# HGRN scores in bursts of two levels, with decayed keys and queries alternating between two pairs of tiles

## The chip, the cores and the metric

The kernel runs on one core of a Trainium2 chip. The metric is the device time of one execution in microseconds. Engines are called as the profile calls them: PE (TensorE, with PEld for its weight loads), DVE (VectorE), ACT (ScalarE), POOL (GpSimd), SP (SyncE, which issues the DMAs).

## The reference

One decoder layer is computed for a prompt of 1024 new tokens and for 8 sequences that decode one token each. RMSNorm, one input projection, then two mixers side by side: HGRN2 (8 heads, key and value width 128) and Mamba-2; an output projection with residual; RMSNorm and a gated MLP; a final RMSNorm. The part that the change touches is one HGRN head over the prompt. With forget gates f, keys k = 1 - f, queries q and values v:

```python
b = jnp.cumsum(g, axis=2)                                  # g = log f
o = jnp.einsum('bhtk,bhkv->bhtv', q * jnp.exp(b), S)
diff = b[:, :, :, None, :] - b[:, :, None, :, :]
decay = jnp.exp(jnp.where(causal, diff, -jnp.inf))
A = jnp.einsum('bhtsk,bhsk->bhts', decay * q[:, :, :, None, :], k)
o = o + jnp.einsum('bhts,bhsv->bhtv', A, v)
S_new = jnp.exp(b_last[:, :, 0])[..., None] * S + jnp.einsum('bhsk,bhsv->bhkv', k * jnp.exp(b_last - b), v)
```

The decay between two positions differs in each of the 128 key channels, so the scores A are no plain product of q and k. All data is float32.

## The kernel before, in words

The layer runs in one program. PE executes in the order in which the program is written; the order of DVE, ACT, POOL and of the DMA queues is made by a planner at build time, which follows data dependencies and takes earlier-written work first. On each engine the instructions then run in that order.

**Two interleaved streams.** Projections are jobs in a list (`in_job`, `out_job`). A job of a head is one of its four inputs f, q, v and sg (the output gate): 3 chunks of 344 columns times 24 matmuls, 72 steps of one matmul, each step a `yield`. A head's recurrence (`head`, L810) is a generator too; it yields weights. `drive` walks through the head's generator and for a weight w runs w x left / 32 steps of the projection jobs, where left is 4 jobs x 72 = 288. While head h is worked on, the four projections of head h+1 run in between; for the last head the output jobs o8.0 to o12.2 run instead, with residual tiles transposed in between. What the generator leaves of the four jobs runs behind its last piece. The weights thus set how many projection matmuls stand between two pieces of a head, and PE keeps that order.

**The scores of one head.** T = 1024 positions lie along the free axis of q, k and f (128 channels on the partitions); they are cut into 8 chunks of 128. Pairs of positions at distance zero, then within blocks of 2, 4, 8, ... are scored level by level. `near` (L851) issues the scores of a level as 32 small matmuls, 32 columns of k by 32 of q, each into a 32-partition strip of a PSUM bank; on PE each is two instructions. `scale(lv)` (L840) then multiplies the first half of every block of 2 x 2^lv keys by the second half's decay, and the second half of the queries by the first half's decay, in place, and forms the decays of the doubled blocks (tiles `tt`). The order written is: a yield of 2 (head 0: 5), the transposes of v (`vtp`, L872), level "a0" with undecayed q; q = q*f on DVE (L876) and the diagonal into `amc` (L877); then for lv = 0 to 3 a score burst `a1`, `scale(lv)` (L845, L846, L848), and a predicated copy of that level's scores into `amc` (L887); inside lv = 3, after two more units, a burst 16 columns wide and `scale(4)`. Then four ACT copies of `amc` into the block matrix `am` (L890), burst `a5` (16 matmuls), `scale(5)` and ACT copies (L896), burst `a6` (8 matmuls of 64 x 64), `scale(6)` and a copy (L902). A level's matmuls read k and q, the next `scale` writes them in place, so each level waits for the one before on PE and on DVE in turn.

**What follows in a head.** `od` is the readout of the eight decode states (its decode states `Sh` are prepared on DVE L828 and POOL L827 and L829, its queries `qb` L819), copied to `odr` (L911). `ktp` transposes the decayed keys (L917), `kv` forms chunk states that DVE accumulates (L929, L931), `o` forms the outputs, `hms` and `dms` their norms. Before all of it stands `vd` (L815), the transpose of v's 8 decode columns, which DVE copies (L817) and SP stores and reloads.

**Buffers.** f, k, q, v and sg are tiles of the ring "big" (10; head 0's f is in "e", 2). Half tiles (`vt`, `kt`, `tt`, `SS`, `sq`, `amc`) come from the ring "s" (11). Score banks come from a ring of four PSUM banks "mx"; `vd`, `od`, `odp`, `dms` and the norm sums `ms` of the Mamba stage share one bank "nx".

**What lies beside it.** Weight tiles are split into a high and a low part on ACT (`wh`, L183) and DVE (`wl`, L184) at each job's start. Projection results leave PSUM through ACT (L799), f further through L792 and k through DVE L793. In head 0 the Mamba gate's norm is still finished on DVE (L638 to L640, L683). In head 7 the mixer outputs are split for the output jobs (L984 on ACT, L985 on DVE) and residuals are added (L769).

Of the kernel before, what the change touches and what calls it, by code (L numbers as in the profile page):

```python
# [12 lines left out]
ALU = mybir.AluOpType  # L13
# [3 lines left out]
P = 128  # L17
# [33 lines left out]
def hybrid_layer(  # L51
# [19 lines left out]
    def nm(s):  # L71
        cnt[0] += 1
        return f"{s}_{cnt[0]}"
# [12 lines left out]
    def half(name):  # L86
        return tl("s", name)[:, :512]
# [722 lines left out]
    def head(h, t):  # L810
        f, k, q, v, sg = (t[n] for n in ("f", "k", "q", "v", "sg"))


        dps = bank("vd", "nx")
        PE.transpose(dps[:ND, :P], v[:, T:NT], ident)  # L815
        vd = small.tile([ND, P], F32, tag="vd", name=nm("vd"))
        V.tensor_copy(vd, dps[:ND, :P])  # L817
        SP.dma_start(vd_d[h], vd)
        V.tensor_tensor(qb[:, :, 0:ND], eye8, q[:, T:NT].unsqueeze(2).to_broadcast([P, ND, ND]), op=ALU.mult)  # L819
        Sds = []  # L820
        for b0 in (0, 4):
            bs = slice(b0, b0 + 4)
            ds = slice(T + b0, T + b0 + 4)
            Sd, vb = tl("ld", "Sh"), tl("d", "vb")[:, :512]
            fetch(d4(Sd), state_hgrn[0, bs, h].rearrange("b k v -> k b v"))
            fetch(vb, vd_d[h, bs].rearrange("b n -> (b n)").unsqueeze(0).to_broadcast([P, 512]))
            G.tensor_tensor(d4(vb), d4(vb), cb(k[:, ds]), op=ALU.mult)  # L827
            V.tensor_tensor(d4(Sd), d4(Sd), cb(f[:, ds]), op=ALU.mult)  # L828
            G.tensor_tensor(Sd, Sd, vb, op=ALU.add)  # L829
            SP.dma_start(hgrn_sample[0, bs, h].rearrange("b k v -> k b v"), d4(Sd))  # L830
            Sds.append(d4(Sd))


        hb = [slice(0, 512), slice(512, T)]
        qa, ka, fa = q[:, :T], k[:, :T], f[:, :T]
        vt, kt, SS, sq = ([None, None] for _ in range(4))
        tts = [half("tt"), half("tt")]
        Tc = fa

        def scale(lv):  # L840
            nonlocal Tc
            hh, nb = 1 << lv, 512 >> lv
            q4, k4 = (t.rearrange("p (n two h) -> p n two h", two=2, h=hh) for t in (qa, ka))
            T3 = Tc.rearrange("p (n two) -> p n two", two=2)
            V.tensor_tensor(k4[:, :, 0, :], k4[:, :, 0, :], T3[:, :, 1:2].to_broadcast([P, nb, hh]), op=ALU.mult)  # L845
            V.tensor_tensor(q4[:, :, 1, :], q4[:, :, 1, :], T3[:, :, 0:1].to_broadcast([P, nb, hh]), op=ALU.mult)  # L846
            Tn = tts[0] if lv == 0 else tts[1][:, 512 - (1024 >> lv):512 - (512 >> lv)]
            V.tensor_tensor(Tn, T3[:, :, 0], T3[:, :, 1], op=ALU.mult)  # L848
            Tc = Tn

        def near(ps, s0, t0, n, step):  # L851

            for c in range(NC):
                for b in range(0, P, step):
                    c0 = c * P + b
                    mm(ps[b + s0:b + s0 + n, c * 32 + t0:c * 32 + t0 + n], k[:, c0 + s0:c0 + s0 + n],
                       q[:, c0 + step - n:c0 + step])

        def c32(t):
            return t.rearrange("p (c t) -> p c t", t=32)  # L860

        def m32(m):
            return m.unsqueeze(1).to_broadcast([P, NC, 32])


        amc = half("amc")[:, :256]
        yield 2.0 if h else 5.0
        for hf in range(2):
            vt[hf] = half("vt")
            ps = bank("vtp")  # L870
            for i in range(4):
                PE.transpose(ps[:, blk[i]], v[:, hf * 512 + i * P:hf * 512 + (i + 1) * P], ident)  # L872
            A.copy(vt[hf], ps)
        ps = bank("a0")
        near(ps, 0, 0, 32, 32)
        V.tensor_tensor(qa, qa, fa, op=ALU.mult)  # L876
        V.tensor_tensor(c32(amc), c32(ps[:, :256]), m32(eyec), op=ALU.mult)  # L877
        yield 2.5
        for lv in range(4):
            ps = bank("a1")  # L880
            near(ps, 0, 0, 32, 32)
            scale(lv)
            if lv == 3:
                yield 2.0
                near(ps, 0, 16, 16, 32)
                scale(4)
            V.copy_predicated(c32(amc), m32(mlow[:, lv, :]), c32(ps[:, :256]))  # L887
            yield 2.2 if lv else 2.6
        for g in range(4):
            A.copy(am[32 * g:32 * g + 32, :, 32 * g:32 * g + 32], c32(amc)[32 * g:32 * g + 32])  # L890

        ps = bank("a5")
        near(ps, 0, 0, 32, 64)
        scale(5)
        for b in (0, 64):
            A.copy(am[b:b + 32, :, b + 32:b + 64], c32(ps[:, :256])[b:b + 32])  # L896
        yield 2.0
        ps = bank("a6")
        for c in range(NC):
            mm(ps[0:64, c * 64:(c + 1) * 64], k[:, c * P:c * P + 64], q[:, c * P + 64:(c + 1) * P])  # L900
        scale(6)
        A.copy(am[0:64, :, 64:P], ps[0:64, :].rearrange("p (c t) -> p c t", t=64))  # L902
        yield 1.8


        ops = bank("od", "nx")
        for b in range(ND):
            g = b % 4
            mm(ops[32 * g:32 * g + 32, :P], qb[:, b, :], Sds[b // 4][:, b % 4, :], start=(b < 4), stop=(b >= 4))
        odr = small.tile([P, P], F32, tag="odr", bufs=1, name=nm("odr"))  # L910
        V.tensor_copy(odr, ops[:, :P])  # L911

        for hf in range(2):
            kt[hf] = half("kt")
            ps = bank("ktp")
            for i in range(4):
                PE.transpose(ps[:, blk[i]], k[:, hf * 512 + i * P:hf * 512 + (i + 1) * P], ident)  # L917
# [525 lines left out]
```

## Time and profile before

| | |
|---|---|
| median of 3 runs | 1794.77 us (1794.24 to 1795.13) |
| the profiled execution | 1793.98 us, span 1791.7 us |
| busy share of the span | PE 97%, PEld 94%, DVE 63%, ACT 44%, POOL 23% |
| the eight heads | about 384 to 900 us of the span |
| one steady head | 62.0 us |

Times in a trace count from the start of the span. A row of the timeline has start, time, engine, line, operation, output tile and input tiles, shapes and count, and in brackets the idle time before it and what ended it. A row of the chain of waits has start, time and what the chain ran through, with a count of instructions. A row of the waits names who waited for whom, the microseconds in total, the times and the longest. A row of the stretches gives busy microseconds of each engine with instruction counts, the granted PE clock and the DMA share. Matmuls are pipelined, so their durations overlap; the distance from start to start is what one costs PE.

### The profile page before, as it was taken

To read this page: it belongs to the slowest core of one execution; us is meant where nothing else is said; L and a number is where in the kernel's file an instruction comes from. 1 tells how busy PE (TensorE), PEld (TensorE's weight loads), DVE (VectorE), ACT (ScalarE), POOL (GpSimd) and SP (SyncE) were. 2 spreads that over 40 slices of the span, in tenths; PEclk is the share of its full clock that TensorE was granted. 3 is DMA by queue.
4 is the path that set the end of the run, shared out by engine and by line. 5 is a ranking of instruction groups with operands and counts; after the bars stand their busy time and mean duration, and the time that the engine had idled before them with its cause. 6 is when DMAs were issued, how large, how long until landed. Compare 5 with 4: busy or idle time off the path is not lost.

```text
span 1791.7 us, 38454 instructions
## 1 busy us (share of the span) xinstructions
PE 1735.9 (97%) x16143; PEld 1678.5 (94%) x16143; DVE 1124.0 (63%) x2011; ACT 793.1 (44%) x1416; POOL 406.7 (23%) x415
## 2 busy tenths in 40 slices
PE   7999999999999999999999988999999999999998
PEld 6998899998999999999899978999999999999997
DVE  6667966565554555557746769666666667555545
ACT  7577688453444344345323344333433334111114
POOL 2113322120110110111100364455444542000001
PEclk9999999999999999999999998999999999999999
DMA  4144734642221222234333431222222225422212
GB/s 154 39 126 125 192 106 126 183 136 97 72 79 50 84 74 70 66 96 149 93 118 121 140 108 48 95 72 72 79 84 87 72 72 198 151 90 96 96 60 95
DMA packets 218019, 182.34 MB, mean 102 GB/s; under 512 B 13388, under 2 KB 195158, under 8 KB 217830
## 3 DMA queue, kind: packets, MB, share of 16 engines
q1 hardware_dynamic: 217558, 179.80, 32.6%
q8 instruction: 126, 2.06, 0.5%
q14 instruction: 47, 0.39, 0.1%
q0 software_dynamic: 288, 0.10, 0.0%
HBM read 141.53 MB, written 38.52 MB: 100 GB/s over the span
## 4 chain that ended last, share of the span: by engine, by line
PE 81%; DVE 7%; ACT 4%; DMA 3%; issue 2%; POOL 1%; SPq 0%; DVEq 0%; POOLq 0%; ACTq 0%
PE mm L93 34%; PE ub L93 14%; PE dn L93 14%; PE ua L93 10%; PE a L93 2%; PE o L93 1%; DMA csb<-cs_d 1%; ACT csb L530 1%; PE kv L93 1%; DVE ml L985 1%; DMA ml<-mix_d 1%; DVE wl L184 1%; DVE xbc L334 1%; DMA ws<-in_w_in_dram 1%; ACT L531 1%
## 5 line engine op out<-in xcount | busy, mean ns | idle before, releaser
L93 PE MATMUL mm<-hh,wh 128*128 128x344 f32 x1248 | 407.6, 327 | 0.0
L93 PE MATMUL mm<-hl,wh 128*128 128x344 f32 x1248 | 405.9, 326 | 0.0
L93 PE MATMUL mm<-hh,wl 128*128 128x344 f32 x1248 | 404.3, 324 | 0.0
L93 PEld LDWEIGHTS mm<-hh,wh 128*128 128x128 f32 x1248 | 236.2, 190 | 3.5 <-issue 0.9
L93 PEld LDWEIGHTS mm<-hl,wh 128*128 128x128 f32 x1248 | 236.2, 189 | 2.6 <-issue 0.9
L93 PEld LDWEIGHTS mm<-hh,wl 128*128 128x128 f32 x1248 | 236.2, 189 | 2.3 <-issue 1.0
L183 ACT CAST wh<-ws 128x1024 fp32r<-128x1024 f32 x96 | 100.5, 1047 | 259.8 <-PE dn L93 130.9
L93 PE MATMUL ub<-ul,wh 128*128 128x258 f32 x704 | 200.1, 284 | 4.3 <-DVE ul L1130 4.3
L93 PE MATMUL ub<-uh,wh 128*128 128x258 f32 x704 | 200.4, 285 | 2.0 <-ACT uh L1129 2.0
L93 PE MATMUL ub<-uh,wl 128*128 128x258 f32 x704 | 200.6, 285 | 0.0
L93 PE MATMUL dn<-ah,wh 128*128 128x256 f32 (+1 forms) x640 | 181.2, 283 | 0.9 <-DVE x L1373 0.9
L93 PE MATMUL dn<-al,wh 128*128 128x256 f32 (+1 forms) x640 | 180.5, 282 | 0.0
L93 PE MATMUL dn<-ah,wl 128*128 128x256 f32 (+1 forms) x640 | 180.1, 281 | 0.0
L184 DVE TENSOR_TENSOR wl<-ws,wh 128x1024 fp32r<-128x1024 f32 x96 | 125.7, 1310 | 49.6 <-ACT wh L183 47.4
L93 PE MATMUL mm<-mh,wh 128*128 128x258 f32 x512 | 148.0, 289 | 9.0 <-DVE x L1026 8.9
L93 PE MATMUL ua<-ul,wh 128*128 128x258 f32 x528 | 149.2, 282 | 0.9 <-DVE ul L1130 0.9
L93 PE MATMUL ua<-uh,wh 128*128 128x258 f32 x528 | 148.8, 282 | 0.0
L93 PE MATMUL ua<-uh,wl 128*128 128x258 f32 x528 | 148.4, 281 | 0.0
L93 PE MATMUL mm<-ml,wh 128*128 128x258 f32 x512 | 146.3, 286 | 0.3 <-DVE ml L985 0.3
L93 PE MATMUL mm<-mh,wl 128*128 128x258 f32 x512 | 146.1, 285 | 0.0
L93 PEld LDWEIGHTS ub<-ul,wh 128*128 128x128 f32 x704 | 134.5, 191 | 5.0 <-DVE ul L1130 5.0
L93 PEld LDWEIGHTS ub<-uh,wh 128*128 128x128 f32 x704 | 134.2, 191 | 2.5 <-ACT uh L1129 2.5
(333 smaller groups left out, 3914.5 us busy)
## 6 DMA issues: line engine op xcount, KB each, us to landing
ws<-in_w_in_dram SPq DMA_DIRECT2D x52, 512.0 KB
ws<-in_w_up_dram SPq DMA_DIRECT2D x44, 512.0 KB
ws<-in_w_out_dram SPq DMA_DIRECT2D x24, 512.0 KB
act_d<-val SPq DMA_DIRECT2D x22, 516.0 KB
al<-act_d SPq DMA_DIRECT2D x22, 516.0 KB
ws<-in_w_down_dram SPq DMA_DIRECT2D x22, 512.0 KB
ml<-mix_d SPq DMA_DIRECT2D x48, 172.0 KB
csb<-cs_d SPq DMA_DIRECT2D x32, 256.0 KB
```

The costliest lines, as they stand in the source:

```text
L93: PE.matmul(out, lhsT, rhs, start=start, stop=stop)
L183: A.copy(wh[:, :n], ws[:, :n])
L184: V.tensor_tensor(wl[:, :n], ws[:, :n], wh[:, :n].bitcast(F32), op=ALU.subtract)
L334: V.scalar_tensor_tensor(acc[:, :n], ext[:, q:q + n], col(wname, q * ntile + j), acc[:, :n], op0=ALU.mult, op1=ALU.add)
L530: A.activation(csb3[:, h, :], csb3[:, h, :], AF.Relu, scale=-1.0, bias=cst[:, h0 + h:h0 + h + 1])
L531: A.activation(csb, csb, AF.Exp, scale=-1.0)
L985: V.tensor_tensor(lo[:, cols], x_, hi[:, cols].bitcast(F32), op=ALU.subtract)
```

## The change

Decayed keys and queries have two pairs of tiles, (k, v) and (f, q). The transposes of v move to the head's start, right behind `vd`, so that v is free; q*f is written to v ahead of the first yield. `scale(lv, x_, y_)` reads pair x_ and writes pair y_; where they differ, ACT copies the halves that are not multiplied. A group of the score stage is now two levels: a0 with level 0, level 1 with level 2, level 3 with its 16-wide part, level 5 with level 6; `od` follows level 6 in the same group. Levels 1, 3 and 5 write to the other pair. `ktp` reads f, which holds the final keys, and stands behind a yield of its own. Six copies of 128 x 512 per head are new on ACT; the numbers of matmuls, of DVE products and of DMAs do not change. The weights of a head sum to 28.2 before and after (head 0: 31.2 and 30.7).

```diff
         PE.transpose(dps[:ND, :P], v[:, T:NT], ident)
+        vt = [half("vt"), half("vt")]
+        for hf in range(2):
+            ps = bank("vtp")
+            for i in range(4):
+                PE.transpose(ps[:, blk[i]], v[:, hf * 512 + i * P:hf * 512 + (i + 1) * P], ident)
+            A.copy(vt[hf], ps)
...
-        Tc = fa
-        def scale(lv):
+        Tc = f[:, :T]
+        pair = [(k[:, :T], v[:, :T]), (f[:, :T], q[:, :T])]
+        def scale(lv, x_, y_):
...
+            V.tensor_tensor(ky[:, :, 0, :], kx[:, :, 0, :], T3[:, :, 1:2].to_broadcast([P, nb, hh]), op=ALU.mult)
+            V.tensor_tensor(qy[:, :, 1, :], qx[:, :, 1, :], T3[:, :, 0:1].to_broadcast([P, nb, hh]), op=ALU.mult)
+            if x_ is not y_:
+                A.copy(ky[:, :, 1, :], kx[:, :, 1, :])
+                A.copy(qy[:, :, 0, :], qx[:, :, 0, :])
...
+        def level(lv, ps):
+            V.copy_predicated(c32(amc), m32(mlow[:, lv, :]), c32(ps[:, :256]))
...
-        yield 2.0 if h else 5.0
+        V.tensor_tensor(pair[0][1], q[:, :T], f[:, :T], op=ALU.mult)
+        yield 2.5 if h else 5.0
+        p0, p1 = bank("a0"), bank("a1")
+        near(p0, (k, q), 0, 0, 32, 32)
+        near(p1, pair[0], 0, 0, 32, 32)
+        scale(0, pair[0], pair[0])
+        scale(1, pair[0], pair[1])
+        V.tensor_tensor(c32(amc), c32(p0[:, :256]), m32(eyec), op=ALU.mult)
+        level(0, p1)
+        yield 4.5
+        p0, p1 = bank("a1"), bank("a2")
+        near(p0, pair[0], 0, 0, 32, 32)
+        near(p1, pair[1], 0, 0, 32, 32)
+        scale(2, pair[1], pair[1])
+        scale(3, pair[1], pair[0])
+        level(1, p0)
+        level(2, p1)
+        yield 4.5
+        ps = bank("a3")
+        near(ps, pair[1], 0, 0, 32, 32)
+        near(ps, pair[0], 0, 16, 16, 32)
+        scale(4, pair[0], pair[0])
+        scale(5, pair[0], pair[1])
+        level(3, ps)
         for g in range(4):
             A.copy(am[32 * g:32 * g + 32, :, 32 * g:32 * g + 32], c32(amc)[32 * g:32 * g + 32])
+        yield 4.5
+        ps, p6 = bank("a5"), bank("a6")
+        near(ps, pair[0], 0, 0, 32, 64)
+        for c in range(NC):
+            mm(p6[0:64, c * 64:(c + 1) * 64], f[:, c * P:c * P + 64], q[:, c * P + 64:(c + 1) * P])
+        scale(6, pair[1], pair[1])
         for b in (0, 64):
             A.copy(am[b:b + 32, :, b + 32:b + 64], c32(ps[:, :256])[b:b + 32])
+        A.copy(am[0:64, :, 64:P], p6[0:64, :].rearrange("p (c t) -> p c t", t=64))
         ops = bank("od", "nx")
...
         V.tensor_copy(odr, ops[:, :P])
+        yield 3.5
...
-                PE.transpose(ps[:, blk[i]], k[:, hf * 512 + i * P:hf * 512 + (i + 1) * P], ident)
+                PE.transpose(ps[:, blk[i]], f[:, hf * 512 + i * P:hf * 512 + (i + 1) * P], ident)
```

More of the change, by code (lines that the diff above doesn't have):

```diff
@@ L834, in head @@
         hb = [slice(0, 512), slice(512, T)]
-        qa, ka, fa = q[:, :T], k[:, :T], f[:, :T]
-        vt, kt, SS, sq = ([None, None] for _ in range(4))
+        kt, SS, sq = ([None, None] for _ in range(3))
         tts = [half("tt"), half("tt")]
-        Tc = fa
-        def scale(lv):
+        Tc = f[:, :T]
+        pair = [(k[:, :T], v[:, :T]), (f[:, :T], q[:, :T])]
+        def scale(lv, x_, y_):
             nonlocal Tc
             hh, nb = 1 << lv, 512 >> lv
-            q4, k4 = (t.rearrange("p (n two h) -> p n two h", two=2, h=hh) for t in (qa, ka))
+            (kx, qx), (ky, qy) = ([t.rearrange("p (n two h) -> p n two h", two=2, h=hh) for t in z] for z in (x_, y_))
             T3 = Tc.rearrange("p (n two) -> p n two", two=2)
-            V.tensor_tensor(k4[:, :, 0, :], k4[:, :, 0, :], T3[:, :, 1:2].to_broadcast([P, nb, hh]), op=ALU.mult)
-            V.tensor_tensor(q4[:, :, 1, :], q4[:, :, 1, :], T3[:, :, 0:1].to_broadcast([P, nb, hh]), op=ALU.mult)
+            V.tensor_tensor(ky[:, :, 0, :], kx[:, :, 0, :], T3[:, :, 1:2].to_broadcast([P, nb, hh]), op=ALU.mult)
[3 more added lines that the diff above has]
+                A.copy(qy[:, :, 0, :], qx[:, :, 0, :])
             Tn = tts[0] if lv == 0 else tts[1][:, 512 - (1024 >> lv):512 - (512 >> lv)]
@@ L849, in scale, with near @@
             Tc = Tn
-        def near(ps, s0, t0, n, step):
+        def near(ps, kq, s0, t0, n, step):
+            kk, qq = kq
             for c in range(NC):
@@ L855, in near @@
                     c0 = c * P + b
-                    mm(ps[b + s0:b + s0 + n, c * 32 + t0:c * 32 + t0 + n], k[:, c0 + s0:c0 + s0 + n],
-                       q[:, c0 + step - n:c0 + step])
+                    mm(ps[b + s0:b + s0 + n, c * 32 + t0:c * 32 + t0 + n], kk[:, c0 + s0:c0 + s0 + n],
+                       qq[:, c0 + step - n:c0 + step])
         def c32(t):
@@ L863, in m32 @@
             return m.unsqueeze(1).to_broadcast([P, NC, 32])
+        def level(lv, ps):
+            V.copy_predicated(c32(amc), m32(mlow[:, lv, :]), c32(ps[:, :256]))
         amc = half("amc")[:, :256]
-        yield 2.0 if h else 5.0
[L868 to L888, printed above, removed]
+        V.tensor_tensor(pair[0][1], q[:, :T], f[:, :T], op=ALU.mult)
@@ L889, in head @@
+        scale(3, pair[1], pair[0])
[8 more added lines that the diff above has]
+        level(3, ps)
         for g in range(4):
             A.copy(am[32 * g:32 * g + 32, :, 32 * g:32 * g + 32], c32(amc)[32 * g:32 * g + 32])
-        ps = bank("a5")
-        near(ps, 0, 0, 32, 64)
-        scale(5)
+        yield 4.5
@@ L895, in head @@
+        ps, p6 = bank("a5"), bank("a6")
[3 more added lines that the diff above has]
+        scale(6, pair[1], pair[1])
         for b in (0, 64):
             A.copy(am[b:b + 32, :, b + 32:b + 64], c32(ps[:, :256])[b:b + 32])
[L897 to L900, printed above, removed]
@@ L901, in head @@
-        scale(6)
-        A.copy(am[0:64, :, 64:P], ps[0:64, :].rearrange("p (c t) -> p c t", t=64))
-        yield 1.8
+        A.copy(am[0:64, :, 64:P], p6[0:64, :].rearrange("p (c t) -> p c t", t=64))
         ops = bank("od", "nx")
```

## The prediction

> **What bounds the kernel now.** I read the page's busy shares first, then the waits of PE, then the chain of waits through one HGRN head, then the timeline of PE at one score burst.
>
> ```profile
> PE 1735.9 (97%) x16143; PEld 1678.5 (94%) x16143; DVE 1124.0 (63%) x2011; ACT 793.1 (44%) x1416; POOL 406.7 (23%) x415
> 646.00:708.00 62.00, 62.00 (x810) 59.30 (x809) 34.63 (x63) 27.30 (x42) 8.27 (x6) 1.00 0.24 71
> PE a L93 <- DVE q L846: 8.2, 4, 4.2
> PE ms L93 <- DVE vd L817: 1.8, 1, 1.8
> ```
>
> The second row is one period of a steady head (columns: PE, PEld, DVE, ACT, POOL busy, granted clock, DMA share): PE is never idle in its 62 us, at full clock, while DVE works 34.6 and ACT 27.3. So in heads 1 to 6 only PE's own time counts. All waits of PE in the eight heads that matter are the last two rows: four for decayed queries (one of 4.2 us in head 0, the others, 4.0 together, in head 7) and one at head 0's start. The chain through this period shows what PE's time is made of:
>
> ```profile
> 641.37 5.52 PE mm L93 x35
> 646.88 0.11 PE vd L815
> ...
> 649.83 0.87 PE vtp L872 x8
> 650.70 0.69 PE a L93 x50
> 651.39 3.66 PE mm L93 x22
> ...
> 682.82 0.57 PE od L93 x16
> 683.39 1.02 PE ktp L917 x8
> ```
>
> An undisturbed projection matmul costs 5.52/35 = 0.158 us. Between them stand ten groups on narrow columns of the array: vd, eight score bursts (a0, shown right behind vtp, and levels 0 to 3, each of 64 instructions; then the 16-wide half, level 5, level 6) and od. What one costs shows in the timeline of PE (start, time, instruction):
>
> ```profile
> 654.57 0.32 PE L93 MATMUL mm<-hh,wl 128*128 128x344 f32 x1
> 654.73 0.32 PE L93 MATMUL mm<-hh,wh 128*128 128x344 f32 x1
> 654.99 0.76 PE L93 MATMUL a<-q,k 128*32 128x32 f32 x64
> 655.68 0.43 PE L93 MATMUL mm<-hl,wh 128*128 128x344 f32 x1
> 655.94 0.32 PE L93 MATMUL mm<-hh,wl 128*128 128x344 f32 x1
> L93 PE MATMUL a<-q,k x3456: 176/196/270, 395.3 to 869.7; 128*32 128x32 f32 x160, 128*16 128x16 f32 x32
> ```
>
> The burst starts 0.26 us after the last projection instead of 0.158 (0.10 lost). Its 64 instructions span 0.76 and each lasts 0.196 (last row, median), so the last starts 0.56 after the first: 0.009 apiece. The next projection starts at 0.69, 0.13 after that, and its successor 0.26 later, 0.10 over the pitch. **The edges of a burst cost 0.10 + 0.13 + 0.10 = 0.33 us, its matmuls 0.56.** A level that joins another's burst saves 0.33.
>
> **The change, part by part.** The matmuls are the same in number and shape. A unit of a yield is 288/32 = 9 projection steps, 1.42 us, and the yields of a head sum to 28.2 units before and after (head 0: 31.2 and 30.7), so only the grouping changes. (2.5 units are 22 steps, as in the row of 22 projections behind a0.)
>
> *Score groups.* Joined are a0 with level 0, level 1 with 2, level 3 with the 16-wide half: 3 x 0.33 = 0.99 us per head. Level 5, level 6 and od also run together, but with the array's columns going 32, 64, 32 inside. The trace has no such direct turn; the nearest are the full group's turns to and from narrow columns:
>
> ```profile
> 649.66 1.04 PE L872 MATMUL vtp<-ident,v 128*128 128x128 f32 x8
> 650.63 0.36 PE L93 MATMUL a<-q,k 128*32 128x32 f32 x20
> ...
> 682.75 0.65 PE L93 MATMUL od<-Sh,qb 128*32 128x128 f32 x16
> 683.32 1.09 PE L917 MATMUL ktp<-ident,k 128*128 128x128 f32 x8
> ```
>
> From 649.66, eight transposes at 0.87/8 = 0.109 would have ended at 650.53; the burst starts at 650.63, so a turn costs 0.10 there. Each of the two joints then saves between 0 (the turn costs a whole edge) and 0.33; I take 0.15, nearer to the 0.10 row with something for the tail: 0.30 per head. Against it, od no longer turns straight into ktp but back to a projection, at 0.13 + 0.10; the present turn takes some 0.2 of the 0.57 between their starts, so I put a loss of 0.06 (0 to 0.33). The vtp transposes move from a0 to vd: both cost 0.87 either way. Sum: 0.99 + 0.30 - 0.06 = **1.23 us per head** (0.7 to 1.6).
>
> The Trainium skill, TensorEngine Tiling, Key Properties, says that changing the tiling mode drains TensorE. The 0.33 agrees with a drain at each change; by that rule the two inner joints change the mode too and save nothing, and the sum would be 2 us smaller over the heads.
>
> *Waits between bursts.* Before, each level waited for PE, then had about 3.4 us. Now two levels have 4.5 units, 6.4 us, and their second half may come 0.26 + 0.56 later: 7.2 us from the end of a burst for two k and two q products, two merges and whatever else DVE does. The rows of the present period, first the stretch that becomes window one (DVE shares it with POOL's decode products), then what falls in window two:
>
> ```profile
> 655.79 1.10 DVE L845 TENSOR_TENSOR k<-k,f 128x512 f32<-128x512 f32 x1 [0.52 <-PE a L93]
> 656.81 1.78 DVE L846 TENSOR_TENSOR q<-q,f 128x512 f32<-128x512 f32 x1
> 660.29 1.11 DVE L845 TENSOR_TENSOR k<-k,tt 128x512 f32<-128x512 f32 x1 [1.34 <-PE a L93]
> 661.33 0.68 DVE L846 TENSOR_TENSOR q<-q,tt 128x512 f32<-128x512 f32 x1
> 661.93 0.44 DVE L887 COPY_PREDICATED amc<-mlow,a 128x256 f32<-128x256 uint8 x1
> 662.83 1.23 DVE L184 TENSOR_TENSOR wl<-ws,wh 128x1024 fp32r<-128x1024 f32 x1 [0.46 <-ACT wh L183]
> 664.47 0.70 DVE L793 TENSOR_SCALAR k<-f 128x1032 f32<-128x1032 f32 x1 [0.41 <-ACT f L792]
> 656.42 1.62 POOL L829 TENSOR_TENSOR Sh<-Sh,vb 128x512 f32<-128x512 f32 x1
> L873 ACT COPY vt<-vtp x16: 586/589/595, 395.0 to 836.8; 128x512 f32<-128x512 f32 x16
> ```
>
> Window one: 1.10 + 1.78 + 1.11 + 0.68 for the products, 2 x 0.44 for the two merges, 0.7 for one product of decays (128x512 too): 6.2 us. Window two: 4 x 0.69, 0.88, 1.23, 0.70: 5.6. Both are under 7.2.
>
> New on ACT are two copies of 128x512 for each of three levels, the halves that the level does not scale. No row has such a strided copy from one buffer to another; the nearest is the 0.59 of vt, so 6 x 0.59 = 3.5 us per head on an engine with 35 us to spare. If one must wait for the DVE product beside it, it ends 0.6 after DVE: 6.8 of 7.2 in window one. That is thin, and I charge 0.3 us per head for it in heads 1 to 6 (0 to 1.2). The product q*f now goes to v, after the transposes of v: emitted 2.5 units (3.5 us) ahead of the burst that reads it; its 1.2 to 1.4 us (twice a 128x512 product) are hidden by those projections, and uncovered would cost as much a head.
>
> Buffers: v and f are held to level 5 and to ktp, k is freed sooner; the ring of ten holds two heads of five tiles, and the next writer comes a head later, so nothing. Decode outputs: od's inputs come from POOL's L829, at work at 656 (the row above), and od moves only from 682.8 to near 676; its earlier copy to odr and selod matmul stay behind kv. No DMA is added, and vd's store and SP's queue keep their place; the vt copies, 1.2 us, stand earlier in ACT's queue, where the next eviction comes a chunk of 24 projections (3.8 us) later.
>
> *Head 0.* Its PE starts with vd and then idles 1.8 us for DVE (the wait of ms above); the vt transposes now fill that hole: 0.88 saved (0 to 0.88). Later level 2's scores wait for level 1's product, with DVE at work without a break:
>
> ```profile
> 393.66 0.52 DVE L638 SCALAR_TENSOR_TENSOR nt<-ms,gacc 128x344 f32<-128x344 f32 x1 [2.71 <-ACT gacc L637]
> 396.76 2.23 DVE q L876
> 405.55 4.82 DVE xbc L683 x4
> 412.33 0.88 PE L93 MATMUL a<-q,k 128*32 128x32 f32 x64 [4.25 <-DVE q L846]
> 413.21 4.39 PE mm L93 x18
> 394.00:460.00 66.00, 61.75 (x808) 58.61 (x810) 41.24 (x71) 30.27 (x45) 7.73 (x5) 0.97 0.23 74
> ```
>
> The 18 projections behind the wait take 4.39 instead of 18 x 0.158 = 2.84, and its burst 0.88 instead of 0.69: after the pause PE ran at a lower clock (0.97 granted over this head, last row, against 1.00 in the steady one), so the stall costs 4.25 + 1.7 = 6.0. In the changed order q*f (1.2 when undisturbed) and 1.5 of the decay products fit into DVE's 2.71 of idle time ahead of 393.66, and level 1's product, which no longer waits for level 1's scores, comes ahead of L683. DVE, done with level 1 at 412.2 now, would be 2.23 + 1.5 earlier: 408.5, with level 2 (2 x 0.68) at 409.8 and level 3 at 411.2, its ACT copy at 411.8. PE's unstalled time for level 2's scores is now 412.33 - 4.25 = 408.1, for level 3's 18 projections and a burst later, 411.8; less two joints (0.66) and the 0.88 it is 410.3, and 411.1 for the 16-wide half. That half is late next, by 0.7. I take 4.0 of the 6.0 (0 to 6.0), since DVE's order is a planner's.
>
> *Head 7.* Three waits for q, 4.0 us, where DVE is crowded by the splits of the output stage:
>
> ```profile
> 849.85 5.31 DVE L985 TENSOR_TENSOR ml<-ml,mh 128x344 fp32r<-128x344 f32 x4
> ```
>
> DVE's total is unchanged and level 2 is due 3 us sooner; level 3 is due at the same step. The stall absorbs the joints before it, and only those behind it count: 0.3 (-3 to 3).
>
> **The sum**, against the profiled execution's 1793.98 us: heads 1 to 6 give 6 x (1.23 - 0.3) = 5.6, head 0 1.23 + 0.88 + 4.0 = 6.1, head 7 0.3: 12.0 us. The median of the runs is 0.8 above the profiled one, so the forecast is 1794.77 - 12.0 = 1782.8.
>
> **Rivals.** *The edges do not merge:* a second level costs its full 0.89 although it follows directly, if the edge is paid for each set of accumulators. For it: no two levels are adjacent in this trace. Against it: the 64 instructions already go to four column groups without a break. Left would be head 0's 4.9 and nothing else: about 1790.
>
> *DVE becomes late in window one.*
>
> ```profile
> L845 DVE TENSOR_TENSOR k<-k,tt x48: 676/692/1704, 410.9 to 870.0; 128x512 f32<-128x512 f32 x48
> L846 DVE TENSOR_TENSOR q<-q,tt x48: 675/684/1778, 411.5 to 870.6; 128x512 f32<-128x512 f32 x48
> ```
>
> If all four products take their maxima beside POOL, they take 2 x (1.70 + 1.78) = 7.0, and with merges and decays 8.5: 1.3 late in each of seven heads, some 9 us, of which 1.8 is charged already. That leaves 1794.8 - 12.0 + 7.3 = 1790. Against it: POOL works 8.3 us of a period, and only part of it falls there.
>
> *A wait on ACT takes the place (the slower side).*
>
> ```profile
> ACT wh L183 <- PE mm L93: 9.6, 4, 4.1
> ```
>
> ACT waits for PE up to 4.1 us at the head of its queue in this period. If a copy is ordered behind such an eviction or cast, the burst that needs it waits too. One such copy in a head, 4.1 late with about 1.3 us of cover, costs 2.8; in seven heads 19.6, which against the 13.8 gained without my 1.8 charge gives 1800.6. It decides from 2.0 us of lateness per head. Against it: the copies are ready 1 to 3 us after a burst, when the queue has mostly drained. The Trainium skill, TensorE: Matmul & The Clock Gate, Engine queue depths, calls ACT's queue strict FIFO; no row here shows ACT passing a waiting instruction either.
>
> *Head 0 and head 7 gain nothing and lose 2:* the joints of head 0 and the hole stay, 1794.8 - 5.6 - 2.1 + 2 = 1789.
>
> **How the numbers follow.** Forecast 0.60; heads 0 and 7 bad 0.10; edges do not merge 0.10; DVE late 0.10; ACT late 0.10. The likeliest case itself runs from 1776 (head 0's stall gone whole, 3 us of head 7's, no charge: 1794.8 - 18.5) to 1788. The range takes 1777 and reaches to 1791, over the 1789 and 1790 cases; the ACT case and the tails of the others are left out, 2 in 10. A measurement tells about 0.2% (3.6 us) from no change: faster takes the forecast, the 1789 case and most of the two near 1790 (0.80), the same takes the rest of these (0.10), slower the ACT case (0.10).
>
> **What would show it.** Four score groups per head in PE's timeline, of 128 instructions spanning about 1.3 us with one pair of edges; a period near 61 us instead of 62; steady heads without a wait for q, k or f; head 0's waits near 1 us instead of 6. Wrong would be rows of PE waiting for the new ACT copies or for DVE in every head, or a gap of 0.3 inside a group.

## The result, and the profile after

The changed kernel takes 1784.63 us in the median of six runs (1782.61 to 1789.39), the kernel before 1795.06 (1794.24 to 1797.23): a ratio of 0.9937, with a 95% interval of 0.9924 to 0.9950. The forecast was 1782.8. The profiled execution of after is the fastest of its six (1782.61 us, span 1780.9), and lies 11.4 us below the profiled execution of before (1793.98), 0.9 more than the medians differ.

Busy times on the page of after, and the waits of PE in the eight heads that matter (who waited for whom, us in total, times, longest; the others are of 0.2 to 0.7 us):

```profile
PE 1725.4 (97%) x16143; PEld 1675.6 (94%) x16143; DVE 1119.3 (63%) x2011; ACT 817.5 (46%) x1464; POOL 405.3 (23%) x415
```
```profile
PE mm L93 <- ACT x L1038: 2.8, 1, 2.8
PE a L93 <- DVE q L854: 2.5, 1, 2.5
PE a L93 <- DVE v L854: 0.7, 1, 0.7
...
PE ms L93 <- DVE vd L823: 0.5, 1, 0.5
```

PE has as many instructions as before and 10.5 us less of busy time: edges of bursts count as busy, so this is where the joints show. ACT has 48 instructions and 24 us more, the copies. The 8.2 us of waits for decayed queries have become 2.5 (head 0) and, in head 7, 0.7 and 0.3 (the early q*f, L882), but a wait that was not there is now the longest: 2.8 us for an ACT eviction, in head 7. A steady head is head 5 (columns as in the prediction):

```profile
699.48:760.21 60.73, 60.73 (x808) 59.19 (x807) 33.93 (x61) 30.41 (x48) 8.23 (x7) 1.00 0.25 72
```

PE is still never idle, at full clock, and the period fell from 61.91 to 60.73. This is what a group looks like in PE's timeline (a0 with level 0):

```profile
703.78 0.32 PE L93 MATMUL mm<-hh,wh 128*128 128x344 f32 x1
704.02 0.73 PE L93 MATMUL a<-q,k 128*32 128x32 f32 x62
704.57 0.20 PE L93 MATMUL a<-v,k 128*32 128x32 f32 x1
...
704.61 0.74 PE L93 MATMUL a<-v,k 128*32 128x32 f32 x62
705.28 0.42 PE L93 MATMUL mm<-hl,wh 128*128 128x344 f32 x1
705.54 0.32 PE L93 MATMUL mm<-hh,wl 128*128 128x344 f32 x1
```

From 703.78 to 705.54 are 1.76 us; less two pitches of 0.158 the group costs 1.44, and two single bursts cost 2 x 0.89 = 1.78. The joint saved 0.34. The second level's first row stands among the first level's last ones: PE runs through the joint without a gap.

Where the time went, head by head (distance of the starts of `vd` in the traces, for head 7 to the last matmul of `hms`; us). Columns: before, after, and five of the runs below.

| head | before | after | joints opened | early q*f alone | copies twice | one joint opened | tail spread |
|---|---|---|---|---|---|---|---|
| 0 | 71.46 | 66.98 | 66.35 | 70.09 | 71.29 | 68.14 | 63.80 |
| 1 | 64.32 | 63.14 | 64.39 | 64.35 | 63.25 | 63.59 | 63.12 |
| 2 | 64.51 | 63.31 | 64.55 | 64.47 | 63.30 | 63.66 | 63.39 |
| 3 | 61.90 | 61.46 | 61.91 | 61.91 | 60.93 | 61.06 | 61.21 |
| 4 | 61.90 | 60.68 | 61.93 | 61.91 | 60.66 | 60.88 | 60.66 |
| 5 | 61.91 | 60.73 | 61.90 | 61.90 | 60.69 | 60.85 | 60.73 |
| 6 | 61.92 | 61.04 | 61.96 | 61.84 | 61.62 | 61.10 | 60.83 |
| 7 | 57.89 | 57.47 | 58.16 | 57.21 | 57.89 | 59.92 | 58.61 |

After against before: head 0 gains 4.48, heads 1 to 6 together 6.10, head 7 0.42; head 0 also began 0.64 earlier. At the up-projection after stands 12.04 us ahead, at the end of the span 10.82: 1.2 us went in the gated MLP, which the change doesn't touch.

Heads 0 and 7 scatter more than the steady ones. The changed kernel's head 0 was 66.98 here, 68.05 in run 9 and 68.14 in run 2 (where it is not edited), its head 7 57.47, 58.51 and 59.92. Against the one trace of before that is a gain of 3.3 to 4.5 us in head 0, and anything from a gain of 0.4 to a loss of 2.0 in head 7.

### The profile page after: what moved, and what is told of

It reads as the page before. It is cut to its first block, busy times and chain, and to the rows that moved or that the text cites. A ratio compares the mean times of both kernels' runs of the same rounds, so it can differ in the third digit from the quotient of the medians.

```text
span 1780.9 us, 38506 instructions
## 1 busy us (share of the span) xinstructions
PE 1725.4 (97%) x16143; PEld 1675.6 (94%) x16143; DVE 1119.3 (63%) x2011; ACT 817.5 (46%) x1464; POOL 405.3 (23%) x415
```

## The experiments

Each time is the median of its runs; the ratio is to runs of the kernel before on the same chip. Lines of an edited kernel may stand a few numbers later than in after.

**1. Joints opened.** All else of the change stays (two pairs, copies, early transposes and q*f); only yields are set between the levels.

```diff
         near(p0, (k, q), 0, 0, 32, 32)
+        yield 2.5
         near(p1, pair[0], 0, 0, 32, 32)
...
         near(p0, pair[0], 0, 0, 32, 32)
+        yield 2.2
         near(p1, pair[1], 0, 0, 32, 32)
```

> The changed kernel with its joints opened: the eight score bursts and od stand where they stood before (2.0, 4.5, 7.1, 9.3, 11.5, 13.5, 15.7, 17.7 and 19.5 units into a head); the two pairs of tiles, the ACT copies and the early v transposes stay. Edge theory (a steady head gains 1.22 us because PE pays fewer turns between wide and narrow matmuls): the steady head goes back from 60.7 to 61.9 us, and seven heads lose 7 to 8.5 us against the changed kernel, so about 1791 to 1793. Rival (the gain comes from levels that no longer wait for each other on DVE): steady heads stay at 60.7 and the time stays near 1784.

Measured: 1790.82 us, ratio 0.9971 (0.9958 to 0.9984). Heads 3 to 6 are back within 0.04 of their former periods, heads 1 and 2 within 0.07. PE waits for no q, k or f in these heads in either kernel, so this is the edges. Head 0 keeps its whole gain, 66.35. So the joints are worth 1.24 us in a steady head, and head 0's gain has another source. There the joints bring nothing on balance: PE's wait behind them is 0.9 us with joints opened and 2.5 in after, and the granted clock over head 0 is 1.00 here and 0.97 in after.

**2. One joint opened in each of four heads:** a0|0 in head 1, 3|16 in head 2, 5|6 in head 4, 6|od in head 5, by a yield of 1.0 taken from the yield behind the group.

> The changed kernel with one joint opened in each of four heads by one unit (9 projections), the next yield a unit shorter: head 1 between a0 and level 0, head 2 between level 3 and its 16-wide half, head 4 between levels 5 and 6, head 5 between level 6 and od. Edge theory: head 1 and head 2 grow by 0.33 us each (63.1 to 63.5, 63.3 to 63.6), heads 4 and 5 by 0.15 to 0.20 (60.7 to 60.9). By the reading that a change of the array's columns inside a group costs a whole edge, heads 4 and 5 do not grow at all. If edges do not merge, none grows.

Measured: one run, 1786.68 us. Against after these heads are longer by 0.45, 0.35, 0.20 and 0.12. The opened joint of head 4 in PE's timeline, first of the opened kernel, then the start of the same group in head 5 of after:

```profile
667.60 0.32 PE L93 MATMUL mm<-hh,wl 128*128 128x344 f32 x1
667.85 0.70 PE L93 MATMUL a<-v,k 128*32 128x32 f32 x32
668.48 0.43 PE L93 MATMUL mm<-hh,wh 128*128 128x344 f32 x1
668.74 0.32 PE L93 MATMUL mm<-hl,wh 128*128 128x344 f32 x1
```
```profile
727.44 0.32 PE L93 MATMUL mm<-hh,wl 128*128 128x344 f32 x1
727.69 0.70 PE L93 MATMUL a<-v,k 128*32 128x32 f32 x32
728.32 1.15 PE L93 MATMUL a<-q,f 128*64 128x64 f32 x16
```

Level 5 by itself costs 668.74 - 667.60 - 0.32 = 0.82. In the group it reaches level 6 at 728.32, 0.88 behind the last projection's start, where a pitch is 0.158: 0.72. With the 0.10 over the pitch with which a burst otherwise begins, here level 6, the joint saved 0.20. The turn to 64 columns is cheaper than the way out to a projection and in again, but not free. Each value is from one trace. In the ten other traces with groups heads 1 and 2 repeat within 0.13 us and heads 4 and 5 within 0.07, so the order (plain joints 0.35 to 0.45, inner ones 0.1 to 0.2) can be read from it, and the 0.12 for the joint of level 6 with od only just. (Heads that were not edited moved more: head 3 stands 0.40 above the 60.66 of its best run, head 0 1.16 and head 7 2.45 above after.)

**3. Copies twice.** Each of the two ACT copies of a level is issued a second time.

```diff
+                A.copy(ky[:, :, 1, :], kx[:, :, 1, :])
+                A.copy(qy[:, :, 0, :], qx[:, :, 0, :])
```

> The changed kernel with each of the six new ACT copies of a head written twice. If the copies lie beside PE's work in steady heads, heads 4 and 5 stay at 60.7 us, and only heads 0 and 7, where ACT holds up DVE's norm and PE's evictions, lose 0.5 to 2 us each: about 1785 to 1788. If the copies stand on the path of every head (a wait on ACT), each of the six heads grows by 0.6 us or more: 1788 to 1795.

Measured: 1787.52 us, ratio 0.9950 (0.9933 to 0.9966). Heads 1 to 5 did not grow: there the copies are hidden, with room for as much again. (Head 6 grew by 0.58, with one of the pauses of the last section.) Head 0 was 4.3 us longer than in after, with PE's wait for q at the third group up from 2.5 to 4.3 and a granted clock of 0.95 over the head instead of 0.97. Not all of that belongs to the copies: 1.6 is the wait of `ms` at the head's start (2.1 instead of 0.5), which lies ahead of any copy, and against the second trace of the changed kernel (68.05) the loss is 3.2. Copies are free only where ACT has nothing due behind them.

**4. Level 1's copies of head 0 on POOL.**

> The changed kernel with the two copies of level 1 in head 0 on POOL instead of ACT. Theory: these two copies (0.68 and 0.69 us) stand in ACT's queue ahead of the table load and root of the Mamba norm, so the norm's last chunk reaches DVE 1.3 us later than it could and PE's wait for level 3 is that much longer: with them on POOL the wait of 2.5 us falls to 1.0 to 1.5, and head 0 from 67.0 to about 65.5 us. Rival (the wait is DVE's amount of work alone): the wait stays at 2.5 us. If POOL's copies are slow or slow DVE down beside them, level 2's scores wait instead and head 0 grows.

Measured: one run, 1782.70 us, head 0 at 66.14. DVE no longer idles ahead of the norm's last chunk (1.65 us in after), and the wait for q at the third group fell from 2.5 to 1.2, but its second half now waits 1.2. The view of waits names a DVE merge for it (`amc`, done at 413.12); by the program these matmuls read what ACT copies into v, done at 413.08, so the copy is the likelier cause. It stands behind this row of ACT:

```profile
410.31 1.28 ACT L799 ACT_TABLE_LOAD   x1 [4.61 <-DMA mix_d<-xbc]
```

The load opens the eviction of head 0's next queries, whose buffer is a Mamba tile that L683 on DVE must finish and a DMA store first. So the norm's tail is in both: it holds DVE, and it holds ACT through the buffer. The two waits together, 2.4 us, are hardly less than the one of 2.5 in after. What the run saves is the clock behind them. Head 0 of after, then of this run (columns as in the prediction):

```profile
383.90:450.88 66.98, 63.83 (x815) 61.29 (x813) 44.17 (x78) 39.37 (x58) 5.78 (x5) 0.97 0.28 89
384.91:451.05 66.14, 62.89 (x815) 60.34 (x813) 45.33 (x79) 38.11 (x57) 7.48 (x7) 1.00 0.29 92
```

In after the granted clock was 0.50 from 411 to 413 us, right behind the pause of 2.5; the third group took 1.86 us there and the 37 projections behind it 6.63. With the clock at 1.00 the same projections took 6.04 in this run, and the group took 1.31 in run 5. So the slow stretch cost after 1.1 us.

**5. Norm tail spread.** The four products of L683 in head 0 are written one per 48 projection steps.

```diff
-                tail()
+                if g:
+                    spread(tail(), 48)
...
+                yield
```

> The changed kernel, with one edit in head 0: the four products that finish the Mamba norm (L683, 4.9 us of DVE) and their stores are written one per 48 projection steps instead of all at once, so that DVE's planner may put the products of levels 2 and 3 between them. Theory (head 0's wait of 2.5 us for q at the third group is DVE working off the whole norm tail ahead of level 2): the wait falls below 0.7, head 0's period from 66.98 to about 63.5 to 64.5 (wait, and PE's lower clock behind it), heads 1 to 7 as they were, 1781 to 1782 us against 1784.6 for the changed kernel. Rival (the wait hangs on the ACT copies of level 1, which stand behind a table load, and not on DVE's length of work): wait 2 to 2.5, head 0 near 67, 1784 to 1785. Rival with the other sign: the later stores of the Mamba tiles hold back buffers that the evictions of head 0's q need; a new wait of 1 to 3 us on ACT or SP in head 0, 1785 to 1788.

Measured: 1780.41 us, ratio 0.9901 (0.9886 to 0.9915). DVE in head 0, after first, then this kernel:

```profile
398.95 0.68 DVE L854 TENSOR_TENSOR q<-v,tt 128x512 f32<-128x512 f32 x1
401.28 0.52 DVE L638 SCALAR_TENSOR_TENSOR nt<-ms,gacc 128x344 f32<-128x344 f32 x1 [1.65 <-ACT gacc L637]
...
403.15 4.90 DVE L683 SCALAR_TENSOR_TENSOR xbc<-xbc,vcol,gacc 128x1032 f32<-128x1032 f32 x4
407.96 0.69 DVE L793 TENSOR_SCALAR k<-f 128x1032 f32<-128x1032 f32 x1
408.57 1.22 DVE L184 TENSOR_TENSOR wl<-ws,wh 128x1024 fp32r<-128x1024 f32 x1
409.70 0.69 DVE L853 TENSOR_TENSOR f<-f,tt 128x512 f32<-128x512 f32 x1
```
```profile
406.24 1.28 DVE L687 SCALAR_TENSOR_TENSOR xbc<-xbc,vcol,gacc 128x1032 f32<-128x1032 f32 x1
...
409.18 0.68 DVE L858 TENSOR_TENSOR f<-f,tt 128x512 f32<-128x512 f32 x1
409.78 0.69 DVE L859 TENSOR_TENSOR q<-q,tt 128x512 f32<-128x512 f32 x1
410.39 0.68 DVE L858 TENSOR_TENSOR k<-f,tt 128x512 f32<-128x512 f32 x1
410.99 0.68 DVE L859 TENSOR_TENSOR v<-q,tt 128x512 f32<-128x512 f32 x1
411.59 0.43 DVE L883 COPY_PREDICATED amc<-mlow,a 128x256 f32<-128x256 uint8 x1
411.92 3.69 DVE L687 SCALAR_TENSOR_TENSOR xbc<-xbc,vcol,gacc 128x1032 f32<-128x1032 f32 x3
```

Three of the four products (3.69 us) now run behind levels 2 and 3, although head 0 began 2.0 us later in this trace. PE's waits in head 0 are gone but for `ms` (1.0), and its period is 63.80 at a granted clock of 1.00, 3.2 less than in after and 4.3 less than in the second trace of the changed kernel. The theory holds.

**6. Both edits of head 0 together** (the spread tail, and level 1's copies on POOL).

> Both edits of head 0 together: the norm tail spread over 48 steps each, and level 1's two copies in head 0 on POOL instead of ACT. If the wait at the third group is DVE's work alone, this is the spread kernel again, within 0.3 us of it. If copies on ACT and the norm tail each hold it up by themselves, only this one loses the wait: head 0 near 63.5 to 64.5 and 1781 to 1782 us, the spread kernel near 1784. If the bound is the ACT table load that waits for the Mamba tile's transfer (1.2 us at the third group's second half when POOL made the copies), that wait stays and head 0 is 65.5 to 66.

Measured: 1783.60 us, ratio 0.9923 (0.9908 to 0.9939); head 0 at 64.00 against 63.80, and PE again waits there for nothing but `ms` (1.3). So in head 0 this is the spread kernel: with the tail out of the way the copies on ACT cost head 0 nothing. The two medians lie 3.2 us apart and not within the 0.3 that was expected; run 12 puts the spread kernel at this run's ratio too.

**7. Early q*f alone,** in the kernel before: transposes behind `vd` and q*f in v ahead of the first yield, one burst to a level, in place.

> The kernel before, with two parts of the change alone: v is transposed right behind vd, and q*f is written to v ahead of the first yield; levels are scaled in place, one burst to a level, no copies. Heads 1 to 6 must stay at 61.9 each by every theory. Head 0 was 71.46 before and 66.35 with the alternating pairs but without groups. If the early product and the filled hole are what helped head 0 there, it is 66 to 67.5 here and the time 1789.5 to 1791. If alternating pairs are needed (level 1's product no longer waits for level 1's scores), head 0 keeps most of its wait of 4.2 us, is 69.5 to 70.6 (only the hole's 0.9 and a part of the product), and the time is 1793 to 1794.

Measured: 1795.32 us, ratio 0.9997 (0.9985 to 1.0009). Head 0 is 70.09, 1.4 less than before, and PE still waits for level 2:

```profile
412.54 0.75 PE L93 MATMUL a<-v,k 128*32 128x32 f32 x64 [3.60 <-DVE v L852]
```

Of the 5.1 us that head 0 gains without joints, 1.4 come from the filled hole and the early product, the other 3.7 from the pairs (one trace each, and head 0 scatters by about 1 us): with a second pair level 1's products are done at 399.6 in after, ahead of the norm's tail, where in place they wait for level 1's scores and end up behind it.

**8 and 9. Head 7's casts on POOL, and the changed kernel again beside it.** The first is the spread kernel with `split_in`'s casts on POOL for the outputs that o8 reads.

```diff
-        A.copy(hi[:, cols], x_)
+        cast(hi[:, cols], x_)
...
-                split_in(hi[k], lo[k], cs)
+                split_in(hi[k], lo[k], cs, G.tensor_copy if r0 == 8 else A.copy)
```

> The kernel with the spread norm tail, and in addition the casts of the first four mixer outputs for the output jobs of head 7 (L1003, 12 casts of 128x344, mh<-ml) on POOL instead of ACT, so that ACT's evictions (L1043) no longer stand behind casts that wait 2 to 3 us for the DMA of ml. Theory (the new wait of 2.8 to 4.0 us of PE for the eviction in head 7 is ACT's order): that wait vanishes, ACT shows no idle time before L1003 around 845 us, and what is left in head 7 is the wait for DVE, which needs the casts too (L1004), 0 to 2 us; head 7 from 58.6 to 55.5 to 57, 1777 to 1779.5 us. Rival (the transfer of ml itself is the bound: the next matmuls need those columns anyway): PE waits for mh or ml instead by the same 3 to 4 us, head 7 stays at 58 to 59, no change against the spread kernel. Rival with the other sign: the casts are slower on POOL (twice the 0.48 of ACT), PE waits 1 to 3 us more for mh, 1781 to 1784.

> The changed kernel itself, unedited, on the same chip as the run beside it, so that the two head-0 and head-7 edits are compared with it there: 1783 to 1787 us, head 0 at 67, heads 4 and 5 at 60.7. If the pause of 0.5 us inside a projection run of head 3 belongs to the program it is here again (61.46); if not, head 3 is near 60.7.

Measured: 1781.31 us, ratio 0.9925 (0.9910 to 0.9939), against 1785.64, ratio 0.9949 (0.9935 to 0.9962), for the changed kernel. The wait for the eviction stayed at 3.4, with head 7 at 57.49, so the theory is out. Here no cast stands right ahead of the eviction, but the change's own two copies of level 3, which wait for DVE:

```profile
841.65 0.62 ACT L861 COPY k<-f 128x512 f32<-128x512 f32 x1 [2.44 <-DVE f L858]
843.32 0.62 ACT L862 COPY v<-q 128x512 f32<-128x512 f32 x1 [1.05 <-DVE q L859]
843.85 0.37 ACT L1043 COPY x<-mm 128x258 f32<-128x258 f32 x1
```

Of use is the comparison: with the spread tail and this edit the kernel is 4.3 us faster than the changed one on one chip, and nearly all of that is head 0 (63.88 against 68.05). The changed kernel's head 3 is 61.36 again.

**10. The casts for o12 on POOL** instead (`r0 == 12`).

> The kernel with the spread norm tail, the casts of the second four mixer outputs (those for o12, which ACT ran from 834 to 854 us in the run before) on POOL, all others back on ACT. Theory (ACT's order is head 7's bound: an eviction behind casts that wait for the DMA of ml): PE's wait for the eviction, 3.4 to 4.0 us, falls below 1.5; what may stay is the eviction behind a level's copy that waits for DVE. Head 7 at 55 to 57, 1777 to 1779.5 us. Rival (DVE's L1004, which needs the casts, holds up DVE in the same way): a wait for q, v or x of 3 to 4 us by DVE in its place, head 7 at 57.5 to 59, 1780 to 1782.

Measured: 1783.04 us, ratio 0.9939 (0.9925 to 0.9952), head 7 at 57.99. The wait is still 3.5, where the theory said below 1.5. The timelines of DVE, ACT and PE there:

```profile
837.65 1.34 DVE L1004 TENSOR_TENSOR ml<-ml,mh 128x344 fp32r<-128x344 f32 x1 [1.24 <-POOL mh L1003]
838.91 1.75 DVE L858 TENSOR_TENSOR f<-f,tt 128x512 f32<-128x512 f32 x1
```
```profile
840.75 0.62 ACT L861 COPY k<-f 128x512 f32<-128x512 f32 x1 [8.58 <-DVE f L858]
841.27 0.37 ACT L1043 COPY x<-mm 128x258 f32<-128x258 f32 x1
```
```profile
841.69 0.39 PE L93 MATMUL mm<-mh,wh 128*128 128x258 f32 x1 [3.52 <-ACT x L1043]
```

ACT has no cast there any more and stands idle for 8.58 us, at the head of its queue the change's own copy k<-f, which waits for DVE; behind it the eviction for which PE waits. DVE in turn had waited 1.24 us for a cast, which on POOL stood behind POOL's product for the decode states (L840, until 837.20). The Trainium skill, TensorE: Matmul & The Clock Gate, Engine queue depths, calls ACT strict FIFO; the trace agrees: it held a ready eviction of 0.37 us behind a copy that was not.

**11. Head 7's copies of levels 1 and 3 on POOL as well.**

> As the run beside it, and in head 7 the two copies of level 1 and the two of level 3 on POOL too, behind its casts. If the change's own copies, which wait for DVE in ACT's queue, hold up the eviction (L1043) by themselves, this run is 1 to 3 us faster than the one beside it. If only the casts did, the two agree within 1 us. If POOL, which runs in order too, now holds the copies behind casts that wait for the DMA, PE waits for k, v, f or q of a level by 2 to 4 us and this run is the slower by that.

Measured: 1783.35 us, ratio 0.9934 (0.9922 to 0.9947), head 7 at 58.12. The 3.5 fell to 1.4, and in its place stand two waits for DVE:

```profile
PE a L93 <- DVE q L859: 1.5, 1, 1.5
PE mm L93 <- ACT x L1044: 1.4, 1, 1.4
...
PE a L93 <- DVE v L859: 1.2, 1, 1.2
```

The sum is nearly the same (4.1 us, and 3.9 for the eviction in run 10). In these two runs the rival of run 10 fits: head 7 waits for DVE with its products, the splits and the casts they need, and taking ACT out of the way moves the wait to another name. That is argued from the waits; what bounds head 7 of after is another matter (see head 7 below).

**12. The spread kernel a second time.**

> The kernel with the spread norm tail, unedited, a second time: its first ratio to the kernel before was 0.9901, while four kernels that share its head 0 and differ in head 7 or in two copies gave 0.9923 to 0.9939, though their traces show the same head 0 (63.4 to 64.0) and head 7 within 1.2 us. If the first ratio belongs to the kernel, it is 0.989 to 0.9915 again. If it was a favourable chip or hour, it is 0.992 to 0.994, which is what the traces' 3 us in head 0 against the changed kernel's 0.9937 to 0.9949 would give.

Measured: 1783.06 us, ratio 0.9925 (0.9908 to 0.9941), head 0 at 64.31. The first ratio was on the good side. The kernel's two ratios lie 0.1% to 0.5% below the changed kernel's two (0.9937 and 0.9949); the 3 to 4 us of head 0 in the traces are 0.2%. It beats the kernel before clearly. Against the changed kernel the second interval overlaps (0.9924 to 0.9950 there), so the gain rests on head 0, which took 63.4 to 64.3 us in all six traces with the spread tail and 67.0 to 68.1 in the three of the changed kernel. Runs 6 and 8, which share the spread tail, are as fast within their intervals.

## Why the prediction was right, point by point

*Score groups, 1.23 us per head:* right, also in its parts. Run 1 gives 1.24 for a steady head (61.90 against 60.66, the period of heads 4 and 5 in most grouped kernels), a plain joint reads 0.34 against 0.33, and an inner one 0.1 to 0.2 against 0.15. The rival that edges don't merge is out. By the rule of the Trainium skill's TensorEngine Tiling, Key Properties, that a change of the tiling mode drains TensorE, inner joints would save nothing, as the prediction read it; the timeline of run 2 shows 0.20 saved where columns go from 32 to 64 (one trace). A turn there does cost something, as the rule has it, but less than the way out and in.

*The thin window, a charge of 0.3 per head:* not needed as a wait. PE has no wait for q, k or f in heads 1 to 6. Window one in head 4 (second group at 651.26, its second half at 651.87):

```profile
645.92 0.68 DVE L853 TENSOR_TENSOR k<-k,f 128x512 f32<-128x512 f32 x1
...
648.82 1.78 DVE L854 TENSOR_TENSOR q<-v,tt 128x512 f32<-128x512 f32 x1
```
```profile
647.80 0.65 ACT L857 COPY q<-v 128x512 f32<-128x512 f32 x1
```

DVE ends at 650.60, 1.27 before it is needed, even with one product slowed to 1.78; the ACT copy ran ahead of that product instead of behind it, so the added 0.6 of the working did not occur. The DVE rival and the ACT rival are out for the steady heads, and run 3 shows that twice the copies change nothing there. The 6 x 1.23 = 7.4 were still not all reached (6.10): 0.8 are missing in head 3 and 0.3 in head 6, where PE paused without waiting for any semaphore (last section). That the sum with the charge, 5.6, came near the 6.1 is luck: the charge stood for a wait that is not there.

*Head 0, 6.1:* mis-sized; 4.48 in the first trace, 3.4 and 3.3 in the two others (68.05 and 68.14). The hole behind `vd` was filled as said, and by more (the wait of `ms` is 0.5 instead of 1.8, though it varies from 0.5 to 2.1 among the kernels run). The term that failed is the 4.0 saved of the stall's 6.0: 2.5 of waiting and 1.1 of lower clock are left in after, so some 2.4 were saved, and head 0's waits are 3.0 us instead of the "near 1" forecast. Two steps of the working are behind it.

The first is "level 2 at 409.8 and level 3 at 411.2": they came at 411.0 and 412.2. The order forecast for level 1, ahead of L683, is what the trace shows (399.6). But DVE then stood idle for 1.65 us, waiting for ACT's norm factor, and ACT had been busy with the change's own two copies ahead of its table load:

```profile
398.13 0.68 ACT L856 COPY f<-k 128x512 f32<-128x512 f32 x1 [1.67 <-DVE v L854]
398.69 0.69 ACT L857 COPY q<-v 128x512 f32<-128x512 f32 x1
399.40 1.28 ACT L637 ACT_TABLE_LOAD   x1
400.70 0.55 ACT L637 ACTIVATE gacc<-ms,epsc 128x344 f32<-128x344 f32 x1
```

The working had put ACT's copies at nothing in head 0 except behind level 3. Run 4 takes the idle time of DVE away by moving them, and run 5 wins 3.2 to 4.3 us by cutting up the 4.9 us of L683 that stood in front of level 2.

The second is PE's time for the third group, "410.3": PE had nothing left to do from 408.6 on. The head began 0.6 earlier in this trace, the hole gave 0.45 more, and the half unit by which head 0's yields shrank (31.2 to 30.7) left 115 projections ahead of that group instead of 119, 0.6 us that the working did not count. As the group starts when DVE is done, what PE saves ahead of it only lengthens the wait. The prediction says so of head 7 ("the stall absorbs the joints before it") but adds the joints of head 0 in full; run 1 shows that they bring nothing there.

The forecast named the right thing as late next (the third group) and was 1.6 to 2.8 too kind to it. In size that is the difference between the forecast and the median, a gain of 10.4 us instead of 12.0, but it is not the whole account: heads 1 to 6 gave 0.5 more than forecast, head 0 began 0.6 earlier, and 1.2 went in the gated MLP.

*Head 7, 0.3:* 0.42, then -0.6 and -2.0 in the other traces; within its -3 to 3, which says little. What was not foreseen is the exchange inside it: DVE's three waits of 4.0 us became 1.1 for DVE's queries and one of 2.8 for ACT. The row of ACT behind which that eviction stands, and PE's wait for it:

```profile
848.78 0.48 ACT L998 CAST mh<-ml 128x344 fp32r<-128x344 f32 x1 [1.01 <-DMA ml<-mix_d]
```
```profile
850.10 0.39 PE L93 MATMUL mm<-mh,wh 128*128 128x258 f32 x1 [2.76 <-ACT x L1038]
```

Between the two stand the copy f<-k (849.16) and the eviction (849.68). The cast waits for the transfer of a mixer output (`ml`), and so do, through earlier casts, the splits on DVE ahead of the product that the copy needs. Runs 8, 10 and 11 moved casts and copies but not that transfer, so whether it is what bounds head 7 of after stays open. The ACT rival had a score burst waiting for a copy that stands behind other work of ACT. That shows in one trace at most, in head 0 of run 4; in head 7 it is an eviction that stands behind the casts and a copy.

## What to carry to other kernels

On an engine that is never idle, count the turns between kinds of work as work: here three turns fewer of 0.33 us and two cheaper ones, in the six steady heads, gave 6.1 of the 10.8 us between the traces, at the price of copies on an engine with room. In a head that waits for another engine the same turns bring nothing until that wait is gone. A copy on a queue that runs in order is free only where nothing behind it is due, so look for the places (a first and a last iteration) where other stages share that queue. A second pair of tiles pays most where it lets an engine run ahead of a fixed block of work, and then the next step is to cut that block up.

## What the runs showed that was not expected

PE paused in head 3 of after at two places without a semaphore wait: in a run of projections (0.54 from start to start), and in the second half of a group (1.10 instead of 0.75):

```profile
587.18 0.32 PE L93 MATMUL mm<-hh,wl 128*128 128x344 f32 x1
587.72 0.43 PE L93 MATMUL mm<-hh,wh 128*128 128x344 f32 x1 [0.22 <-issue]
```
```profile
590.28 0.76 PE L93 MATMUL a<-v,k 128*32 128x32 f32 x64
590.89 1.10 PE L93 MATMUL a<-q,f 128*32 128x32 f32 x64
```

The pause in the group comes again at nearly the same step in the second trace (14.2 us into head 3, against 14.3), in the spread kernel (14.1) and in run 8 (14.5), and in head 6, 13.9 to 14.4 us into it, in runs 2, 3, 6, 8, 10 and 11. Of the eleven traces with groups, ten show a pause in head 3 or head 6 (run 4 is the one without, and its head 3 is 60.66); the three with single bursts (before, runs 1 and 7) show none there. That points to grouped instructions but does not show it, as run 7 has a pause of 1.06 us of the same kind in head 7. Whether the delivery of instructions to PE is the cause was not tried and stays open. It costs up to 1 us.

Stages that no edit touches moved by more than many edits did: head 0 began between 383.3 and 386.7 us, and six runs of the changed kernel span 6.8 us. Differences under 2 us had to be read from periods of heads, not from times.
